# Down weight sums in whole rows of tiles behind two steps of each recurrent head, token sums in the gate's tile, operand parts in one tile

## The chip, the cores and the metric

The kernel runs on one core of a Trainium2 chip. The metric is the device time of one execution in microseconds, from three runs whose median is given. The core has TensorE (matrix products into PSUM), VectorE (DVE in the rows), ScalarE (ACT), GpSimd (POOL) and SyncE (SP), whose queue issues nearly all DMAs of this kernel. Each engine takes its instructions in the order in which the program holds them.

## The reference

One layer of a streaming encoder, for 1024 prompt tokens and 64 sample tokens, 1088 together, width 1024. The inputs are projected by `w_in`; eight recurrent heads (HGRN2) and eight differential-attention heads work on the projections; a gated mix, a norm, a convolutional feed-forward part and a second norm follow.

```python
hq, hf, hi, hog, dq, dk, dv, g_hg, g_da = _split_in(x @ w_in)
f = lb_hk + (1.0 - lb_hk) * jax.nn.sigmoid(hf)        # forget gate
s_new, o = _hgrn2(q, 1.0 - f, hi, log(f), hg_s0)      # S_t = diag(f_t) S_{t-1} + k_t v_t^T, o_t = S_t^T q_t
y_hg = _rms_norm(o, hg_norm_g) * jax.nn.sigmoid(hog)
y_da = _rms_norm(_diff_attend(dq, dk, dv, lam, mask), subln_g) * (1.0 - lam_init)
m = jax.nn.sigmoid(g_hg) * (y_hg @ w_br_hg) + jax.nn.sigmoid(g_da) * (y_da @ w_br_da)
h = _layer_norm(DEEPNORM_ALPHA * x + m @ w_out, ln1_g, ln1_b)
up = h @ w_up                                         # 1024 -> 2 x 2816
val, gate = jnp.split(conv_b + sum(conv_w[j] * buf[:, j:j + T] for j in range(3)), 2, axis=-1)
out = _layer_norm(DEEPNORM_ALPHA * h + (jax.nn.silu(gate) * val) @ w_down, ln2_g, ln2_b)
```

## The kernel before

Every float32 product is computed as three products of rounded parts: an operand is split into a high part (`ScalarE`, a cast) and a low part (`VectorE`, a subtraction), lines 85 and 86 for weights, and high x high, high x low and low x high are accumulated in PSUM (lines 181, 154 and 1225). A weight load `wraw` is 128x512 in one of three buffers.

The work runs in stages. First x is read and transposed (`load_x`). Then the eight recurrent heads run in a loop (`hgrn`): four projections each (L181), decay factors at four block levels (`lvl`), a base level, whose last VectorE step is L435 (Qp times q), the copies of the base products into `att` (L441), the state products U (L463), the states (L471), the outputs (L490, L493), a norm, and the output gate, whose last VectorE step is L508; the head's output is stored by L509. TensorE works on the next head's projections while a head's chain of VectorE, ScalarE and GpSimd steps runs.

The products `up` and `down` of the feed-forward part use a scheme with seven products of half-size blocks instead of eight. It needs sums and differences of weight blocks and of token blocks. For `down` the four weight combinations named 5, 7, 6 and 3 are made ahead, in `down_sums`, and kept in scratch memory in HBM (`s_w`). There are 22 blocks of 128x256: per block four loads into `ws` tiles (four buffers), four VectorE operations (L525, L527, L529, L532), four stores. After each of the first six heads up to four blocks are called; `tc.issue_after(last.ins)` ties their DMAs in SyncE's queue behind the head's store L509, since the context ties only the instructions on the engine of the instruction it is given. The fourth load of a block follows the block's third store in the program.

After the attention heads and the mix comes `ffn`. Feature tiles f = 0 and 1 are computed as plain products; the tiles from 2 on by `seven_products`, whose results go into a tile `u` (two buffers) through `put` (L166, L168). `conv` reads `u`, writes two `c` tiles (two buffers): `val` and `gate`. Its first lines call `edges`, in which GpSimd zeroes and fills the edge columns of `u` (L1075, L1077). Then the product of the two is stored in `s_act`, and token differences are made for `down`: for f below 11 one difference is written into the first half of `u` and stored in `s_t` (L1130, L1135).

`down` takes its operands through `parts`: a load from scratch memory into the low part's tile, a cast (L1180), a subtraction (L1181); high and low parts are two tags of 15 buffers each, allocated after the 16 result tiles `z`.

The order of instructions on each engine is not written by hand: a planner at build time runs the program on a modelled timeline, takes what is ready by its place in the program, and adds a wait wherever a tile or its memory is reused. `issue_after` adds an order without a wait. Pools that follow one another share memory; `reuse_waits="tile"` makes a new tile wait for those old tiles only whose addresses it takes.

Of the kernel before, what the change touches and what calls it, by code (L numbers as in the profile page):

```python
# [10 lines left out]
F32 = mybir.dt.float32  # L11
F32R = mybir.dt.float32r
I32 = mybir.dt.int32
AF = mybir.ActivationFunctionType
ALU = mybir.AluOpType
# [5 lines left out]
P = 128  # L21
# [5 lines left out]
H = 8  # L27
DFF = 2816
NF = DFF // P
# [16 lines left out]
HF, HT, HD = NF // 2, T // 2, D // 2  # L46
# [7 lines left out]
class K:  # L54
# [282 lines left out]
    def hgrn(self, h, mm, sc, xs, hp, w0=None):  # L337
        nc, a, o = self.nc, self.a, self.o
        w = a["w_in"][0]
        c = h * P  # L340
        V, S, G = nc.vector, nc.scalar, nc.gpsimd
# [92 lines left out]
        G.tensor_tensor(X, X, k, ALU.mult)  # L434
        V.tensor_tensor(Qp, Qp, q, ALU.mult)  # L435
        for g in range(2):
# [70 lines left out]
        V.scalar_tensor_tensor(oT, oT, self.hgg, sq, ALU.mult, ALU.mult)  # L507
        V.tensor_tensor(oT, oT, gt, ALU.mult)  # L508
        return nc.sync.dma_start(self.s_yh[c:c + P, :], oT)  # L509


    def down_sums(self, hp, blocks):
        nc, V = self.nc, self.nc.vector
        w = self.a["w_down"][0]
        CW = HD // 2
        for n in blocks:
            rows, cols = slice(n // 2 * P, n // 2 * P + P), slice(n % 2 * CW, n % 2 * CW + CW)

            def load(i, j):
                t = hp.tile([P, CW], F32, tag="ws", name=self.nm("ws"), bufs=4)  # L520
                r0, c0 = j * HF * P + n // 2 * P, i * HD + n % 2 * CW
                nc.sync.dma_start(t, w[r0:r0 + P, c0:c0 + CW])
                return t
            a21, a22, a11 = load(1, 0), load(1, 1), load(0, 0)
            V.tensor_tensor(a22, a21, a22, ALU.add)  # L525
            nc.sync.dma_start(self.s_w["5"][rows, cols], a22)
            V.tensor_tensor(a21, a11, a21, ALU.subtract)  # L527
            nc.sync.dma_start(self.s_w["7"][rows, cols], a21)
            V.tensor_tensor(a11, a22, a11, ALU.subtract)  # L529
            nc.sync.dma_start(self.s_w["6"][rows, cols], a11)  # L530
            a12 = load(0, 1)
            V.tensor_tensor(a12, a12, a11, ALU.subtract)  # L532
            nc.sync.dma_start(self.s_w["3"][rows, cols], a12)

# [301 lines left out]
    def run(self, stop=99):  # L836
# [3 lines left out]
        with top:  # L840
# [25 lines left out]
            if True:  # L866
                with ExitStack() as es:
# [20 lines left out]
                    for h in range(self.dbg.get("nh", H) if stop != 2 else 0):  # L888
                        last = self.hgrn(h, mm, sc, xs, hp, w0 if h == 0 else None)
                        if h < H - 1:  # L890
                            with tc.issue_after(last.ins):
                                self.down_sums(hp, range(4 * h, min(4 * h + 4, 2 * HF)))
            if stop < 2:
# [162 lines left out]
    def ffn(self):  # L1056
# [11 lines left out]
        def new_u(f):  # L1068
            u = up.tile([P, 2, W], F32, tag="u", name=self.nm("u"), bufs=2)
            return u  # L1070

        def edges(f, u):
            for i in range(2):
                j = f + i * NF
                G.memset(u[:, i, 0:2], 0.0)  # L1075
                for r in range(2):
                    G.tensor_copy(u[:, i, TP + 2 + r:TP + 3 + r],  # L1077
                                  par[:, self.o_st + r * 44 + j:self.o_st + r * 44 + j + 1])

        def put(u, c):  # L1080
# [18 lines left out]
        def weights(f):  # L1099
            return self.seven_weights(a["w_up"][0], f * P, (f + NF) * P)  # L1100

        def conv(f, u):
            c = []
            edges(f, u)
            for i in range(2):
# [22 lines left out]
            def less(dst, src):  # L1128
                for sl, vs in pieces:
                    V.tensor_tensor(dst[:, sl], val[:, vs], src[:, sl], ALU.subtract)  # L1130

            t2, t3 = (u[:, i, :HT] for i in range(2))
            if f < HF:
                less(t2, val)
                nc.sync.dma_start(self.s_t["5"][r], t2)  # L1135
                return
            nc.sync.dma_start(t2, self.s_t["5"][r])
# [39 lines left out]
        def parts(n, f, hi, lo):  # L1177
            raw = lo.bitcast(F32)
            nc.sync.dma_start(raw, operand(n, f))
            S.copy(hi, raw)  # L1180
            V.tensor_tensor(lo, raw, hi.bitcast(F32), ALU.subtract)  # L1181
            return hi, lo
        for f in range(2, NF):
            u, w = new_u(f), weights(f)
            self.seven_products([(w, self.xop[c], put(u, c)) for c in range(2)], up)
            conv(f, u)
            if f == NF - 2:
                for i, e in enumerate(early):
                    parts("1", i, *e)
# [76 lines left out]
        both = ((0, QW), (QW, QW))  # L1266

        z = {n: [ap.tile([P, HT], F32, name=f"z{n}{j}") for j in range(HJ)] for n in ("11", "22", "12", "21")}
        later = []
        for n in DOWN:  # L1270
            x = list(early) if n == "1" else []
            for f in range(len(x), HF):
                x.append(parts(n, f, *[ap.tile([P, HT], F32R, tag="o" + t, name=self.nm("o" + t), bufs=15)
                                       for t in "hl"]))
            if n == "4":
# [77 lines left out]
```

## Time and profile before

| | us |
|---|---|
| median of three runs (lowest to highest) | 2369.62 (2367.26 to 2377.26) |
| the profiled execution | 2376.17 |
| its span, first to last instruction | 2374.3 |
| TensorE busy in the span | 2310.8 |
| VectorE, ScalarE, GpSimd busy | 1578.8, 1061.2, 514.5 |
| mean granted clock of TensorE, as a share of full speed | 0.992 |

Times in rows are microseconds unless marked ns. A stretch row gives from:to, its length, the busy time and count of instructions of PE (matrix products), PEld (weight loads of TensorE), DVE, ACT and POOL, the granted TensorE clock as a share of 2.4 GHz, the busy share of the DMA engines and GB/s moved. A row of waits gives engine and line, what ended the wait, total, number of times, longest. A row by line gives the shape and count, then busy us and mean ns of one, then the engine's idle time just before, with what ended it. A row in order of time gives start, length, engine, line, what was written from what, and in brackets the idle time before it with its end. A row of DMAs gives the number, KB of each and median us from issue to landing. A busy TensorE is not TensorE at its peak, since ends of products are modelled; spans on GpSimd are rough.

### The profile page before, as it was taken

The page shows a single profiled execution, that of the slowest core. Times are in us where ns is not written, and L with a number is a line of the kernel's source. Part 1 is how long each engine was busy: PE and PEld are TensorE (multiplying, and loading weights), DVE is VectorE, ACT ScalarE, POOL GpSimd, SP SyncE. Part 2 cuts the span into 40 slices and gives each one's busy share as a digit, 9 for nine tenths or more (in the row PEclk, how much of TensorE's full clock was granted, in tenths as well). Part 3 has the DMA queues.
Part 4 walks back from the last instruction along what each step waited for, and adds up shares of the span by engine and source line. Part 5 has one row for each costly group of instructions (what it writes and reads, how often), then busy time and mean ns, then how long its engine had stood idle before and what let it go on. Part 6 is the DMA issues. An engine that isn't in the chain of part 4 may idle for free.

```text
span 2374.3 us, 42425 instructions
## 1 busy us (share of the span) xinstructions
PE 2310.8 (97%) x16270; PEld 2254.5 (95%) x16270; DVE 1578.8 (66%) x2788; ACT 1061.2 (45%) x1929; POOL 514.5 (22%) x576
## 2 busy tenths in 40 slices
PE   8999999999999999999999999999999999999998
PEld 8989998999999999999999899999999999999998
DVE  3675655776376655556556756568998888885667
ACT  3444443444344444344344744335644444454346
POOL 2222212222331211201201000012454444410001
PEclk9999999999999999999999999999999999999999
DMA  4132323321433323323323767444433345567665
GB/s 129 35 113 88 98 83 103 111 82 45 135 119 106 98 78 85 92 77 102 91 78 108 240 191 220 136 133 141 149 115 110 100 136 162 161 210 231 214 201 163
DMA packets 389234, 300.83 MB, mean 127 GB/s; under 512 B 23739, under 2 KB 358231, under 8 KB 389030
## 3 DMA queue, kind: packets, MB, share of 16 engines
q1 hardware_dynamic: 384294, 293.36, 40.7%
q10 hardware_dynamic: 4224, 4.46, 0.5%
q8 instruction: 128, 2.10, 0.4%
q0 software_dynamic: 512, 0.29, 0.1%
q14 instruction: 76, 0.62, 0.1%
HBM read 203.70 MB, written 81.75 MB: 120 GB/s over the span
## 4 chain that ended last, share of the span: by engine, by line
PE 80%; DVE 6%; DMA 5%; ACT 3%; issue 3%; POOL 1%; SPq 1%; DVEq 0%; POOLq 0%; ACTq 0%
PE mm L181 40%; PE mm L154 17%; PE mm L1225 10%; PE s L668 3%; PE av L709 2%; DMA ws<-w_down 2%; PE wt L703 1%; DMA s_w<-ws 1%; DMA gb<-s_g 1%; DVE wlo L86 1%; PE o L490 1%; DMA ydl<-s_yd 1%; PE nat L333 1%; PE o L493 1%; PE lv L407 1%
## 5 line engine op out<-in xcount | busy, mean ns | idle before, releaser
L181 PE MATMUL mm<-x,whi 128*128 128x362 f32 (+1 forms) x3456 | 878.2, 333 | 5.4 <-DMA wraw<-w_in 2.4
L181 PEld LDWEIGHTS mm<-x,whi 128*128 128x128 f32 x3456 | 614.3, 190 | 10.9 <-ACT x L311 4.8
L181 PE MATMUL mm<-x,wlo 128*128 128x362 f32 (+1 forms) x1728 | 573.1, 333 | 0.0
L86 DVE TENSOR_TENSOR wlo<-wraw,whi 128x512 fp32r<-128x512 f32 (+1 forms) x420 | 308.6, 740 | 194.5 <-ACT whi L85 190.7
L85 ACT CAST whi<-wraw 128x512 fp32r<-128x512 f32 (+1 forms) x420 | 254.7, 611 | 404.7 <-PE mm L181 197.3
L181 PEld LDWEIGHTS mm<-x,wlo 128*128 128x128 f32 x1728 | 328.0, 190 | 2.0 <-issue 1.0
L1225 PE MATMUL mm<-ol,whi 128*128 128x272 f32 (+2 forms) x608 | 174.6, 289 | 1.1 <-DVE ol L1181 1.1
L1225 PE MATMUL mm<-oh,wlo 128*128 128x272 f32 (+2 forms) x608 | 174.0, 288 | 0.0
L1225 PE MATMUL mm<-oh,whi 128*128 128x272 f32 (+2 forms) x608 | 172.8, 290 | 1.0 <-ACT oh L1180 1.0
L1225 PEld LDWEIGHTS mm<-ol,whi 128*128 128x128 f32 x608 | 114.3, 188 | 1.3 <-DVE ol L1181 1.3
L1225 PEld LDWEIGHTS mm<-oh,whi 128*128 128x128 f32 x608 | 113.3, 188 | 1.2 <-ACT oh L1180 1.2
L1225 PEld LDWEIGHTS mm<-oh,wlo 128*128 128x128 f32 x608 | 114.3, 188 | 0.0
L559 POOL TENSOR_TENSOR rs<-rs,mhalf 128x4 f32<-128x4 f32 (+1 forms) x24 | 22.5, 939 | 373.5 <-DVE rs L558 373.5
L595 POOL TENSOR_TENSOR KL<-kT,B 64x512 fp32r<-64x512 f32 x32 | 48.8, 1526 | 218.2 <-DVE B L594 193.5
L85 ACT CAST whi<-wsum 128x512 fp32r<-128x512 f32 x80 | 49.5, 620 | 95.6 <-PE mm L154 75.0
L668 PE MATMUL s<-B,A 128*128 128x512 f32 (+3 forms) x384 | 87.7, 354 | 3.4 <-ACT E L689 1.6
L168 DVE TENSOR_TENSOR u<-mm,p 128x272 f32<-128x272 f32 (+2 forms) x160 | 55.0, 367 | 45.3 <-PE mm L154 44.2
L387 POOL TENSOR_TENSOR P<-X,k 128x544 f32<-128x544 f32 (+1 forms) x32 | 56.0, 1754 | 129.8 <-ACT X L381 84.6
L704 ACT COPY wT<-wt 128x512 f32<-128x512 f32 (+1 forms) x96 | 46.3, 482 | 80.9 <-PE wt L703 80.3
L709 PE MATMUL av<-dvn,wT 128*128 128x128 f32 x576 | 80.0, 275 | 1.3 <-ACT wT L704 1.3
L1113 DVE SCALAR_TENSOR_TENSOR c<-u,par,c 128x1090 f32<-128x1090 f32 x44 | 79.3, 1802 | 0.7 <-ACT c L1110 0.4
L181 PE MATMUL mm<-ydh,whi 128*128 128x272 f32 x256 | 74.2, 291 | 3.7 <-ACT whi L85 3.7
(392 smaller groups left out, 5986.7 us busy)
## 6 DMA issues: line engine op xcount, KB each, us to landing
wraw<-w_in SPq DMA_DIRECT2D x144, 256.0 KB, 2.9
wraw<-w_up SPq DMA_DIRECT2D x124, 256.0 KB, 3.2
wraw<-w_br_hg SPq DMA_DIRECT2D x48, 256.0 KB, 3.7
ol<-s_t SPq DMA_DIRECT2D x44, 272.0 KB, 5.3
ws<-w_down SPq DMA_DIRECT2D x88, 128.0 KB, 2.9
s_w<-ws SPq DMA_DIRECT2D x88, 128.0 KB, 2.3
s_act<-c SPq DMA_DIRECT2D x22, 512.0 KB, 3.4
s_t<-u SPq DMA_DIRECT2D x33, 272.0 KB, 3.2
```

Source lines behind the costliest of these rows:

```text
L85: nc.scalar.copy(hi[:, :kn, :], raw[:, :kn, :])
L86: nc.vector.tensor_tensor(lo[:, :kn, :], raw[:, :kn, :], hi[:, :kn, :].bitcast(F32), ALU.subtract)
L154: nc.tensor.matmul(ps, l, r, start=(first and k == 0 and i == 0), stop=(k == 3 and i == 2), skip_group_check=not first)
L168: V.tensor_tensor(dst, ps[:, sl], d[other][:, sl], ALU.add)
L181: nc.tensor.matmul(ps[:, :cw], l, r[:, :cw], start=(k == 0 and i == 0), stop=(k == n - 1 and i == 2))
L387: G.tensor_tensor(pk, xv[:, :, :hb], blocks(k, B)[:, :, :hb], ALU.mult)
L595: G.tensor_tensor(kl[r], kT[r, sl], b[r, m, :].bitcast(F32), ALU.subtract)
L668: nc.tensor.matmul(dst[:, kc * 512:kc * 512 + kw], A[i // 2][:, p, m, qc], B[kc][:, m, :kw], start=(p == 0), stop=(p == 1))
L704: S.copy(wT[:, g * 4:g * 4 + nb, :], ps[:, :nb * P].rearrange("p (n e) -> p n e", e=P))
L709: self.last_av = nc.tensor.matmul(av[:, i % n4, :], wT[:, kb, :], vn[:, kb, :], start=(kb == 0), stop=(kb == i))
L1113: V.scalar_tensor_tensor(t[:, :W - 2], u[:, i, 1:W - 1], par[:, self.o_w1 + j:self.o_w1 + j + 1], t[:, :W - 2], ALU.mult, ALU.add)
L1225: nc.tensor.matmul(ps, l, r[:, c0:c0 + cw], start=(k == 0 and i == 0), stop=(k == HF - 1 and i == 2))
```

## The change

Three things are edited. `down_sums` works on a row of 128x512 tiles instead of 128x256 blocks, 11 rows; the four loads stand first, the four adds are made under `issue_after` of a VectorE step, and the four stores follow. `hgrn` returns two such steps, `mid` (the product L435) and `end` (the product L508); the first row of a head is tied behind `mid`, the second behind `end`. The DMAs are no longer tied. In `ffn` the edge columns of `u` are filled where the tile is made, which is now before the preceding convolution, and for f below 11 the token difference is written into the gate's `c` tile and not into `u`. In `down` the high and low parts of an operand share one tile of 15 buffers, and the result tiles `z` are allocated after the first operands.

```diff
--- before.py
+++ after.py
@@ -432,7 +432,7 @@
         S.activation(Qp, X, AF.Exp)
         S.activation(X, X, AF.Exp, scale=-1.0)
         G.tensor_tensor(X, X, k, ALU.mult)
-        V.tensor_tensor(Qp, Qp, q, ALU.mult)
+        mid = V.tensor_tensor(Qp, Qp, q, ALU.mult)
         for g in range(2):
             ps = sc.tile([P, 4, P], F32, tag="sc", name=self.nm("bs"))
             for i in range(4):
@@ -505,32 +505,29 @@
             S.activation(sq[:, c0:c0 + cw], ms[:, :cw], AF.Ln, bias=self.eps)
         S.activation(sq, sq, AF.Exp, scale=-0.5)
         V.scalar_tensor_tensor(oT, oT, self.hgg, sq, ALU.mult, ALU.mult)
-        V.tensor_tensor(oT, oT, gt, ALU.mult)
-        return nc.sync.dma_start(self.s_yh[c:c + P, :], oT)
-
-
-    def down_sums(self, hp, blocks):
+        end = V.tensor_tensor(oT, oT, gt, ALU.mult)
+        nc.sync.dma_start(self.s_yh[c:c + P, :], oT)
+        return mid, end
+
+
+    def down_sums(self, hp, n, behind):
+
         nc, V = self.nc, self.nc.vector
         w = self.a["w_down"][0]
-        CW = HD // 2
-        for n in blocks:
-            rows, cols = slice(n // 2 * P, n // 2 * P + P), slice(n % 2 * CW, n % 2 * CW + CW)
-
-            def load(i, j):
-                t = hp.tile([P, CW], F32, tag="ws", name=self.nm("ws"), bufs=4)
-                r0, c0 = j * HF * P + n // 2 * P, i * HD + n % 2 * CW
-                nc.sync.dma_start(t, w[r0:r0 + P, c0:c0 + CW])
-                return t
-            a21, a22, a11 = load(1, 0), load(1, 1), load(0, 0)
+        rows = slice(n * P, (n + 1) * P)
+        t = {}
+        for i, j in ((1, 0), (1, 1), (0, 0), (0, 1)):
+            t[i, j] = hp.tile([P, HD], F32, tag="ws", name=self.nm("ws"), bufs=4)
+            r0 = j * HF * P + n * P
+            nc.sync.dma_start(t[i, j], w[r0:r0 + P, i * HD:(i + 1) * HD])
+        a11, a21, a12, a22 = t[0, 0], t[1, 0], t[0, 1], t[1, 1]
+        with self.tc.issue_after(behind.ins):
             V.tensor_tensor(a22, a21, a22, ALU.add)
-            nc.sync.dma_start(self.s_w["5"][rows, cols], a22)
             V.tensor_tensor(a21, a11, a21, ALU.subtract)
-            nc.sync.dma_start(self.s_w["7"][rows, cols], a21)
             V.tensor_tensor(a11, a22, a11, ALU.subtract)
-            nc.sync.dma_start(self.s_w["6"][rows, cols], a11)
-            a12 = load(0, 1)
             V.tensor_tensor(a12, a12, a11, ALU.subtract)
-            nc.sync.dma_start(self.s_w["3"][rows, cols], a12)
+        for k, x in (("5", a22), ("7", a21), ("6", a11), ("3", a12)):
+            nc.sync.dma_start(self.s_w[k][rows], x)
 
 
     def gates(self, mm, gp, js):
@@ -886,10 +883,9 @@
                         G.memset(t, 0.0)
                         self.att.append(t)
                     for h in range(self.dbg.get("nh", H) if stop != 2 else 0):
-                        last = self.hgrn(h, mm, sc, xs, hp, w0 if h == 0 else None)
-                        if h < H - 1:
-                            with tc.issue_after(last.ins):
-                                self.down_sums(hp, range(4 * h, min(4 * h + 4, 2 * HF)))
+                        steps = self.hgrn(h, mm, sc, xs, hp, w0 if h == 0 else None)
+                        for n, behind in zip(range(2 * h, min(2 * h + 2, HF)), steps):
+                            self.down_sums(hp, n, behind)
             if stop < 2:
                 return
             mm = top.enter_context(tc.tile_pool(name="mm_d", bufs=2, space=PSUM, reuse_waits="tile"))
@@ -1067,15 +1063,13 @@
 
         def new_u(f):
             u = up.tile([P, 2, W], F32, tag="u", name=self.nm("u"), bufs=2)
-            return u
-
-        def edges(f, u):
             for i in range(2):
                 j = f + i * NF
                 G.memset(u[:, i, 0:2], 0.0)
                 for r in range(2):
                     G.tensor_copy(u[:, i, TP + 2 + r:TP + 3 + r],
                                   par[:, self.o_st + r * 44 + j:self.o_st + r * 44 + j + 1])
+            return u
 
         def put(u, c):
             def f(row, half):
@@ -1101,7 +1095,6 @@
 
         def conv(f, u):
             c = []
-            edges(f, u)
             for i in range(2):
                 j = f + i * NF
                 G.tensor_copy(cst[:, 0:2, j], u[:, i, TP:TP + 2])
@@ -1128,12 +1121,12 @@
             def less(dst, src):
                 for sl, vs in pieces:
                     V.tensor_tensor(dst[:, sl], val[:, vs], src[:, sl], ALU.subtract)
+            if f < HF:
+                less(gate, val)
+                nc.sync.dma_start(self.s_t["5"][r], gate[:, :HT])
+                return
 
             t2, t3 = (u[:, i, :HT] for i in range(2))
-            if f < HF:
-                less(t2, val)
-                nc.sync.dma_start(self.s_t["5"][r], t2)
-                return
             nc.sync.dma_start(t2, self.s_t["5"][r])
             nc.sync.dma_start(t3, self.s_act[r, HT:T])
             less(t2, t2)
@@ -1180,10 +1173,13 @@
             S.copy(hi, raw)
             V.tensor_tensor(lo, raw, hi.bitcast(F32), ALU.subtract)
             return hi, lo
+        u = new_u(2)
         for f in range(2, NF):
-            u, w = new_u(f), weights(f)
+            w = weights(f)
             self.seven_products([(w, self.xop[c], put(u, c)) for c in range(2)], up)
-            conv(f, u)
+
+            u, done = new_u(f + 1) if f < NF - 1 else None, u
+            conv(f, done)
             if f == NF - 2:
                 for i, e in enumerate(early):
                     parts("1", i, *e)
@@ -1264,14 +1260,15 @@
         def tiles(c0, cw):
             return [(r, min(P, c0 + cw - r)) for r in range(c0, c0 + cw, P)]
         both = ((0, QW), (QW, QW))
-
-        z = {n: [ap.tile([P, HT], F32, name=f"z{n}{j}") for j in range(HJ)] for n in ("11", "22", "12", "21")}
         later = []
         for n in DOWN:
             x = list(early) if n == "1" else []
             for f in range(len(x), HF):
-                x.append(parts(n, f, *[ap.tile([P, HT], F32R, tag="o" + t, name=self.nm("o" + t), bufs=15)
-                                       for t in "hl"]))
+                t = ap.tile([P, 2, HT], F32R, tag="o", name=self.nm("o"), bufs=15)
+                x.append(parts(n, f, t[:, 0], t[:, 1]))
+            if n == "1":
+
+                z = {n: [ap.tile([P, HT], F32, name=f"z{n}{j}") for j in range(HJ)] for n in ("11", "22", "12", "21")}
             if n == "4":
                 break
             for j in range(HJ):
```

## Rows read from the trace of the kernel before

**Rows 1.** The page, busy time of each engine over the whole span.

```profile
PE 2310.8 (97%) x16270; PEld 2254.5 (95%) x16270; DVE 1578.8 (66%) x2788; ACT 1061.2 (45%) x1929; POOL 514.5 (22%) x576
```

**Rows 2.** Busy time by stretch: recurrent heads, the products of up, those of down.

```profile
126.00:478.00 352.00, 333.56 (x2203) 320.16 (x2202) 230.21 (x361) 147.81 (x202) 78.46 (x39) 0.98 0.33 100
40.00:126.00 86.00, 85.54 (x566) 83.58 (x565) 44.93 (x64) 37.71 (x49) 19.69 (x9) 1.00 0.14 40
478.00:640.00 162.00, 160.14 (x1053) 155.69 (x1052) 90.74 (x133) 71.17 (x100) 40.29 (x23) 0.99 0.25 76
1735.00:2120.00 385.00, 385.00 (x3064) 385.00 (x3063) 328.82 (x509) 169.43 (x256) 159.92 (x253) 1.00 0.42 133
2130.00:2350.00 220.00, 220.00 (x1759) 219.77 (x1758) 145.89 (x261) 105.70 (x206) 4.99 (x10) 1.00 0.70 220
```

**Rows 3.** Who waited for whom, TensorE, 125 to 530 us.

```profile
PE U L463 <- DVE att L441: 9.8, 3, 5.0
PE nat L333 <- DVE vT L348: 7.9, 10, 2.0
```

**Rows 4.** Groups by line, VectorE, 125 to 530 us.

```profile
L525 DVE TENSOR_TENSOR ws<-ws,ws 128x256 f32<-128x256 f32 x22 | 13.7, 623 | 26.8 <-DMA ws<-w_down 20.1 <-issue 6.7
L527 DVE TENSOR_TENSOR ws<-ws,ws 128x256 f32<-128x256 f32 x22 | 9.1, 416 | 3.6 <-DMA ws<-w_down 2.7 <-DVE att L420 0.7 <-DVE ws L525 0.2
L379 DVE TENSOR_TENSOR X<-b 128x512 f32<-128x512 f32 x6 | 4.1, 690 | 0.1
```

**Rows 5.** Instructions in order of time, VectorE and TensorE, around 170 us.

```profile
169.67 0.43 DVE L525 TENSOR_TENSOR ws<-ws,ws 128x256 f32<-128x256 f32 x1 [4.75 <-DMA ws<-w_down]
172.00 2.07 PE L463 MATMUL U<-vn,kn 128*128 128x128 f32 x8 [4.99 <-DVE att L441]
```

**Rows 6.** Busy time by stretch, right after four gaps of TensorE.

```profile
172.00:178.00 6.00, 6.00 (x23) 5.37 (x24) 4.72 (x14) 0.00 (x0) 0.00 (x0) 0.51 0.41 125
317.80:321.20 3.40, 3.40 (x14) 3.40 (x15) 3.29 (x10) 0.00 (x0) 0.00 (x0) 0.51 0.39 131
366.00:369.20 3.20, 3.20 (x15) 3.02 (x14) 1.96 (x6) 0.00 (x0) 1.34 (x1) 0.53 0.83 227
577.00:580.40 3.40, 3.40 (x16) 3.40 (x16) 3.40 (x5) 0.00 (x0) 0.00 (x0) 0.54 0.00 0
```

**Rows 7.** Busy time by stretch: from one end step to the last state step.

```profile
126.00:177.00 51.00, 45.19 (x298) 42.64 (x297) 42.10 (x66) 19.27 (x29) 10.40 (x5) 0.94 0.40 122
```

**Rows 8.** DMA issues on the page, KB each, median us to landing.

```profile
wraw<-w_in SPq DMA_DIRECT2D x144, 256.0 KB, 2.9
ws<-w_down SPq DMA_DIRECT2D x88, 128.0 KB, 2.9
s_w<-ws SPq DMA_DIRECT2D x88, 128.0 KB, 2.3
```

**Rows 9.** Who waited for whom, ScalarE, 125 to 530 us.

```profile
ACT whi L85 <- PE mm L181: 39.0, 24, 5.5
```

**Rows 10.** Instructions in order of time, SyncE's queue and TensorE, at the start.

```profile
11.64 1.88 SPq L71 DMA_DIRECT2D wraw<-w_in  x2
24.09 0.53 PE L181 MATMUL mm<-x,whi 128*128 128x362 f32 x1 [2.38 <-DMA wraw<-w_in]
```

**Rows 11.** Instructions in order of time, three engines, 1706 to 1714 us.

```profile
1706.33 0.39 PE L154 MATMUL mm<-t3h,whi 128*128 128x272 f32 x1 [1.36 <-DVE p L161]
1711.75 1.30 ACT L1110 ACTIVATE c<-u,par 128x1090 f32<-128x1090 f32 x1 [1.48 <-DMA s_act<-c]
1712.43 0.10 POOL L1075 MEMSET u<- 128x2 f32 x1 [1.55 <-DMA s_t<-u]
1713.37 0.39 PE L154 MATMUL mm<-b11h,whi 128*128 128x272 f32 x1 [2.25 <-ACT u L166]
```

**Rows 12.** Busy time by stretch: after that gap, and where down begins.

```profile
1713.40:1717.40 4.00, 4.00 (x20) 4.00 (x21) 4.00 (x11) 1.35 (x3) 4.00 (x8) 0.57 0.14 44
2120.00:2130.00 10.00, 7.93 (x61) 7.49 (x61) 10.00 (x14) 8.22 (x13) 0.00 (x0) 1.00 1.00 349
```

## The prediction

> **What bounds the kernel now.** Read the page's busy times first: TensorE is busy for 2310.8 us of the 2374.3 us span [rows 1], so all that a reordering can win is some 63 us of TensorE's idle time, plus whatever it loses at its lower clock level. The second view is the table by stretch, to see where that idle time lies. In the stretch from 126 to 478 us, five heads, TensorE is busy for 333.56 of 352 us, 18.44 idle; in the recurrent work before and after it (40 to 126, 478 to 640 us), where few or no Down sums run, it idles 0.46 + 1.86 = 2.32 us in 248. In the long runs of the up and the down products (385 and 220 us) it idles nothing at all [rows 2]. So nothing done inside those two runs can help, and what can help sits in the recurrent heads and at the two seams.
>
> Third, the waits. In the heads TensorE waits 9.8 us for VectorE's copy into att and 7.9 us for its vT copies [rows 3]. Fourth, the groups by line say what VectorE was doing: the first of the four Down sums, L525, has 26.8 us of VectorE's idle time in front of it, 20.1 of it for its loads from w_down [rows 4]. VectorE takes its instructions in the order in which they stand, so a sum whose rows have not landed holds up the recurrence behind it. Fifth, the order in time shows one such case whole: L525 sat for 4.75 us on a load at 169.67, and TensorE's U product then started after a gap of 4.99 us [rows 5]. After the larger gaps the granted clock falls: 0.51, 0.51 and 0.53 after three gaps in this stretch (mostly the 1.2 GHz level instead of 2.4), and 0.54 after one in a head without sums [rows 6].
>
> **The change part by part.**
>
> *Down sums.* The loads lose their place behind the head's last store. Only the four adds are now tied, and only in VectorE's queue: one set behind L435, one behind L508. A set's loads may go out as soon as the four ws tiles are free, that is when the set before it has been stored. Half a head, some 30 to 40 us, lies between two sets; a store lands in 2.3 us and a load in 2.9 [rows 8], so I expect no add to wait for a load. What that wins: the 18.44 us idle less what the clean heads would have in as long a stretch, 352 x 2.32/248 = 3.3, is 15.1 us. The clock: (1-0.51) x 6.0 + 0.49 x 3.4 + 0.47 x 3.2 = 6.1 us lost after gaps here, less the clean share 0.46 x 3.4 x 352/248 = 2.2 [rows 6], is 3.9 us.
>
> What it adds: 44 adds of 128x512 at 0.69 us (L379 has that shape) replace 88 of 128x256 at 0.42 to 0.62 [rows 4], so VectorE's work falls from about 42 to 30 us. But four adds in a row behind L508 hold the next head's first differences for 4 x 0.69 = 2.8 us, in five heads. At worst all of it reaches TensorE, 14 us; at best none. In the stretch of one head VectorE is busy 42.1 of 51 us and TensorE 45.2 [rows 7]; taking out sixteen sums of 0.42 us and putting back 2.8 leaves VectorE 38.2, so 7 us of product work still covers it. I take 0.4 us a head, 2 us. The set behind L435 falls where VectorE waits for TensorE anyway; if that cover is gone, it delays the att copy by up to 2.8 us in each of six heads, 17 us, and I take nothing, as the adds stand later in the program than the head's own steps and fill gaps. Together -15.1 - 3.9 + 2 = -17 us. Bounds: -19 with no burst cost, -4 when most of the two burst costs come through.
>
> The DMAs count too: 44 loads and 44 stores of 256 KB replace 88 and 88 of 128 KB, same bytes; a 256 KB load lands in the same 2.9 us as a 128 KB one [rows 8], so SyncE's queue has half as many issues. Weight loads of the heads stand in that queue behind stores that wait for adds. ScalarE's weight split waits for TensorE (39.0 us, 24 times) and not for a load in these heads [rows 9], so weights lie ready and I cost it at nothing; without that cover it is the slower rival below.
>
> The first set has nothing before it, so its four loads (1.05 MB) may go out while the inputs are still arriving. There a weight load issued at 11.64 us was used at 24.09, TensorE having waited 2.38 us for it [rows 10], 12 us instead of 2.9. This load's tile is free from the start and stands earlier in the program, so the new loads go behind it: 0 us; if ahead, 1.05 MB at the 133 GB/s of the up stretch [rows 2] is 7.9 us. The Trainium skill (DMA: Bandwidth & Descriptors, Queues, rings and completion order) says that each DMA engine consumes its descriptors in ring order; that 12 us landing agrees, and by this rule four loads put ahead cost the weight load their whole transfer, -13.6 instead of -21.5 in the sum below.
>
> *First token sums in the gate's tile, edges one step earlier.* At the seam into the paired products TensorE stands 1.36 us and 2.25 us; the second time it waits for a copy into u, while POOL waits for the store s_t from u, and ScalarE for a c tile [rows 11]. The next 4 us run at 0.57, 1.7 us lost [rows 12]. With the sum in the gate's tile, u is free once the convolution has read it, before that store. But the gate's c tile is now held for two subtractions and a store (2.3 to 2.9 us, rows 8), and the second convolution's ScalarE step waits for a c tile already. Gain at most 1.36 + 2.25 + 1.7 = 5.3 us; loss, if the held tile is what ScalarE stands at ahead of the copy, up to 4 us (store and subtractions). I take 2.25 + 1.7 less 1 for the held tile: -3. After that TensorE has no gap to win, and POOL, 160 of 385 us busy there [rows 2], has room for the earlier edges: 0.
>
> *Operand parts in one tile, z afterwards.* In 2120 to 2130 us TensorE is busy 7.93 us, VectorE 10.00 [rows 12]. The operand tiles move to the lowest addresses, over operands of the last up product that are read first, so their loads can start before that product ends. Gain at most 2.07 us, loss as much if an early load holds the queue. I take -1.5.
>
> **Sum.** -17 - 3 - 1.5 = -21.5 us on the profiled execution, 2376.2 to 2354.7; that execution lies 6.6 us above the median of the runs, so 2348 us. Its own range: -29 (all three gains whole, clean heads without clock dips) to -13, 2341 to 2357.
>
> **Rivals.**
>
> *The waits stay, in part.* A clean head still shows a gap followed by 0.54 [rows 6], and the bursts cost. If half the gain in the heads comes (-8.5) and the seams give 1.5, the time is 2376.2 - 10 - 6.6 = 2360 us. For: VectorE is the busiest engine behind TensorE there. Against: 26.8 us of its standing still goes [rows 4].
>
> *The change doesn't separate loads from adds.* If the adds of one set run just ahead of the next gate, store and load (2.3 + 2.9 = 5.2 us) lie between them and VectorE stands as before, eleven times. Then only the seams gain: 2365 to 2370 us. Against: half a head between the gates.
>
> *The first loads go ahead of the weights at the start.* It decides in which order SyncE's queue takes them: if the four loads stand before the one issued at 11.64 us, TensorE's wait of 2.38 us [rows 10] grows by the 7.9 us worked out above, and the time is 2348 + 8 = 2356 us. For: they wait for nothing. Against: they stand late in the program.
>
> *Slower: SyncE's queue.* Each set's stores wait in SyncE's queue for adds behind a late VectorE step, with the heads' weight loads behind them. It decides once the queue stands longer than the weights are ahead. Then every set costs a landing of 2.9 us [rows 8] and the two passes of the split, as long as a 128x512 add of 0.69 us [rows 4], 4.3 x 11 = 47 us, less 21.5: +25, 2395 us. Against: the split never waited for a load [rows 9], though stores waited for sums in that queue then too.
>
> **How the numbers follow.** Forecast 0.50, waits stay 0.20, first loads ahead 0.08, no separation 0.12, slower 0.10. A change under 0.5% (12 us) can hardly be told from none in this kernel, whose three runs lie 10 us apart. 2357.8 us is the border for faster: the forecast's case, two thirds of the first loads' and a little of the waits' make 0.57; slower is the last case less the part that stays under 2381.5 us, 0.09; the rest 0.34. The range 2338 to 2368 holds the forecast, the waits' and the first loads' cases and half of no separation.
>
> **What would show it.** Right: VectorE's idle time ahead of the first sum under 3 us instead of 26.8; TensorE's wait for att under 3 instead of 9.8; those five heads with less than 6 us idle; the gap of 2.25 at the up seam gone; 2120 to 2130 full. Wrong: sums that still wait for loads; splits that wait for wraw; a longer wait for the third weight tile at the start; a new gap at the second convolution's first step; the copies of vT late behind four adds in a row.

## The result, and the profile after

The changed kernel takes 2356.71 us (median of 5 runs, 2352.85 to 2360.26), the kernel before 2371.3 us (median of 5, 2367.26 to 2377.26): ratio 0.9936, 95% interval 0.9915 to 0.9956. It is faster, by 14.6 us. Forecast was 2348 us, with a range of 2338 to 2368. The profiled executions, 2376.2 us before and 2356.7 after, lie 19.5 us apart: that of before is 5 us above its kernel's median, that of after is on it. The page's first row, after, answers to [rows 1]:

```profile
PE 2303.1 (98%) x16270; PEld 2247.3 (95%) x16270; DVE 1579.6 (67%) x2744; ACT 1056.8 (45%) x1925; POOL 507.9 (22%) x576
```

The same 16270 matmuls take 7.7 us less, at a higher clock; the other 11.7 of the 19.4 us by which the span is shorter were idle time.

The heads first. Busy time by stretch, after (stretch, its length, then busy time and instructions of TensorE, its weight loads, VectorE, ScalarE, GpSimd, then TensorE's clock, DMA share, GB/s):

```profile
126.00:478.00 352.00, 345.29 (x2324) 334.54 (x2323) 244.71 (x335) 157.19 (x214) 80.52 (x41) 1.00 0.32 100
478.00:640.00 162.00, 158.42 (x1031) 153.15 (x1030) 83.72 (x119) 62.00 (x94) 50.34 (x33) 0.98 0.26 80
2101.00:2111.00 10.00, 7.92 (x61) 7.49 (x60) 9.71 (x13) 8.03 (x12) 0.00 (x0) 1.00 0.99 344
```

The 18.44 us idle of [rows 2] are 6.71, and the clock there is 1.00 instead of 0.98. The end of the last recurrent head, told by the first kT transposition behind it, comes at 624.01 us instead of 641.66: 17.65 us of the 19.5. Who waited, TensorE, and the sums by line, VectorE, both 125 to 530 us:

```profile
PE nat L333 <- DVE vT L348: 7.4, 11, 0.8
```

```profile
L528 DVE TENSOR_TENSOR ws<-ws,ws 128x512 f32<-128x512 f32 x10 | 10.5, 1050 | 0.2
L525 DVE TENSOR_TENSOR ws<-ws,ws 128x512 f32<-128x512 f32 x10 | 6.8, 682 | 0.0
```

The wait for att of [rows 3] is gone, and so are the 26.8 us ahead of the first sum [rows 4]. What stays is the wait for vT, in small pieces. The order in time around one head's end shows why; VectorE, then TensorE:

```profile
202.27 0.68 DVE L525 TENSOR_TENSOR ws<-ws,ws 128x512 f32<-128x512 f32 x1
...
205.35 0.68 DVE L526 TENSOR_TENSOR ws<-ws,ws 128x512 f32<-128x512 f32 x1
...
209.02 0.52 DVE L348 COPY vT<-mm 128x364 f32<-128x364 f32 x1
209.47 0.68 DVE L527 TENSOR_TENSOR ws<-ws,ws 128x512 f32<-128x512 f32 x1
...
211.34 0.52 DVE L348 COPY vT<-mm 128x362 f32<-128x362 f32 x1
211.78 1.40 DVE L528 TENSOR_TENSOR ws<-ws,ws 128x512 f32<-128x512 f32 x1
...
213.71 0.52 DVE L348 COPY vT<-mm 128x362 f32<-128x362 f32 x1
```

```profile
211.91 0.55 PE L333 MATMUL nat<-ident,vT 128*128 128x128 f32 x3 [0.77 <-DVE vT L348]
214.28 0.66 PE L333 MATMUL nat<-ident,vT 128*128 128x128 f32 x4 [0.57 <-DVE vT L348]
```

All four adds of the second set stand ahead of the last copy of vT, and each transposition waits for its copy.

The seams, where one stage meets the next, gave nothing. At the up seam (TensorE; ScalarE; SyncE's queue), the answer to [rows 11]; L1103 is the first step of the convolution, L1110 before, and L1115 the store of s_act:

```profile
1687.01 0.40 PE L154 MATMUL mm<-t3h,whi 128*128 128x272 f32 x1 [1.37 <-DVE p L161]
...
1714.47 0.36 PE L154 MATMUL mm<-t4h,whi 128*128 128x272 f32 x1 [1.54 <-DVE u L168]
...
1753.81 0.39 PE L154 MATMUL mm<-t3h,whi 128*128 128x272 f32 x1 [1.30 <-DVE p L161]
```

```profile
1711.29 1.30 ACT L1103 ACTIVATE c<-u,par 128x1090 f32<-128x1090 f32 x1 [5.43 <-DMA s_act<-c]
...
1714.70 1.30 ACT L1103 ACTIVATE c<-u,par 128x1090 f32<-128x1090 f32 x1 [1.32 <-DMA s_t<-c]
```

```profile
1693.59 13.42 SPq L97 DMA_DIRECT2D wraw<-w_up  x3
1707.10 0.46 SPq L1115 DMA_DIRECT2D s_act<-c  x1
```

The gap of 2.25 us is gone, with the low clock behind it (1.00 from 1680 to 1760 us, 0.98 before); gaps of 1.54 and 1.30 us (and one of 0.21) have come. Together the gaps are 4.4 us, 3.6 before. ScalarE now stands 5.43 us for a store that left SyncE's queue at 1707.10, behind three weight loads that waited for their tiles. At the down seam (TensorE) nothing has moved: 2.07 us idle in 10 before [rows 12], 2.08 after, in the same two gaps. TensorE before, then after:

```profile
2122.33 0.77 PE L1225 MATMUL mm<-oh,whi 128*128 128x272 f32 x4 [0.99 <-ACT oh L1180]
2124.18 0.39 PE L1225 MATMUL mm<-ol,whi 128*128 128x272 f32 x1 [1.08 <-DVE ol L1181]
```

```profile
2103.41 0.77 PE L1221 MATMUL mm<-o,whi 128*128 128x272 f32 x4 [0.99 <-ACT o L1173]
2105.26 0.40 PE L1221 MATMUL mm<-o,whi 128*128 128x272 f32 x1 [1.09 <-DVE o L1174]
```

### The profile page after: what moved, and what is told of

The parts are those of the page before. It is cut to its first block, busy times and chain, and to the rows that moved or that the text cites. A ratio compares the mean times of both kernels' runs of the same rounds, so it can differ in the third digit from the quotient of the medians.

```text
span 2354.9 us, 42194 instructions
## 1 busy us (share of the span) xinstructions
PE 2303.1 (98%) x16270; PEld 2247.3 (95%) x16270; DVE 1579.6 (67%) x2744; ACT 1056.8 (45%) x1925; POOL 507.9 (22%) x576
## 4 chain that ended last, share of the span: by engine, by line
PE 82%; DVE 6%; DMA 3%; issue 2%; ACT 2%; POOL 2%; SPq 0%; POOLq 0%; DVEq 0%; ACTq 0%
PE mm L181 43%; PE mm L154 15%; PE mm L1221 10%; PE s L665 3%; PE av L706 3%; PE lv L407 1%; PE wt L700 1%; DVE wlo L86 1%; PE nat L333 1%; DMA gb<-s_g 1%; PE o L490 1%; DMA ydl<-s_yd 1%; PE o L493 1%; PE avd L751 1%; POOL sg L363 1%
## 5 line engine op out<-in xcount | busy, mean ns | idle before, releaser
L1221 PE MATMUL mm<-o,whi 128*128 128x272 f32 (+2 forms) x1216 | 231.2, 289 | 2.1 <-DVE o L1174 1.1
L1221 PEld LDWEIGHTS mm<-o,whi 128*128 128x128 f32 x1216 | 191.0, 188 | 2.6 <-DVE o L1174 1.3
L1221 PE MATMUL mm<-o,wlo 128*128 128x272 f32 (+2 forms) x608 | 174.6, 288 | 0.0
L1221 PEld LDWEIGHTS mm<-o,wlo 128*128 128x128 f32 x608 | 114.2, 188 | 0.0
L665 PEld LDWEIGHTS s<-B,A 128*128 128x128 f32 x384 | 65.9, 190 | 12.1 <-DVE wlo L86 2.1
L102 POOL TENSOR_TENSOR wsum<-wraw,wraw 128x512 f32<-128x512 f32 x40 | 69.1, 1727 | 36.2 <-DVE wlo L86 35.2
```

Source lines behind the costliest of these rows:

```text
L102: G.tensor_tensor(t, x, y, op)
L665: nc.tensor.matmul(dst[:, kc * 512:kc * 512 + kw], A[i // 2][:, p, m, qc], B[kc][:, m, :kw], start=(p == 0), stop=(p == 1))
L1221: nc.tensor.matmul(ps, l, r[:, c0:c0 + cw], start=(k == 0 and i == 0), stop=(k == HF - 1 and i == 2))
```

## The experiments

Each was timed in turns with the kernel before on the same chip; a ratio is to that kernel, with its 95% interval. "Heads" is TensorE's busy time in the 352 us from 126 to 478 (333.56 before, 345.29 changed). A product at the lower clock is busy for longer, so where the clock of that stretch differs it is given too. The planner orders all steps anew for each kernel; no run holds the rest of its order fixed.

**One part at a time.** The Down sums alone (their two functions and the call, as in the diff):

> The kernel before with the Down sums of the change alone; the convolution and the operand tiles as before. Theory: nearly the whole gain of the change is made in the recurrent heads, 17 to 18 us by the end of head 7 as in the profile of the changed kernel, so about 2354 to 2357 us against 2371, and the changed kernel's other two parts are worth 0. Rival: the other two parts gave some of it (3 + 1.5 us, as forecast), or took some back; then this kernel is 3 us or more away from the changed one's 2356.7, above or below.

Measured: 2355.05 us, 0.9918 (0.9906 to 0.9930), heads 345.33. The whole gain: no less than the whole change's.

The convolution's edits alone (`less(gate, val)` and `new_u` a step earlier):

> The kernel before with the first token sums in the gate's tile and the earlier edges alone. Theory: 0, 2371 plus or minus 2 us: the gap of 2.25 us behind the copy into u goes, but two others of 1.3 to 1.5 us come, because ScalarE's first convolution step waits for the store s_act, which stands in SyncE's queue behind a third weight load, and VectorE's work piles up behind it. Rival, as forecast: the held tile costs 1 us only, 3 us are won, 2368.

Measured: 2375.38 us, 1.0008 (0.9997 to 1.0019). TensorE's waits, 1660 to 1775 us, of this kernel:

```profile
PE mm L154 <- DVE u L168: 3.3, 2, 3.1
PE mm L154 <- DVE p L161: 2.7, 2, 1.4
```

Before, it waited there 2.3 us for u and 1.4 for p. The waits have changed their lines and grown by 2.3 us, and the clock falls behind the longest of them, 3.15 us up to 1726.57:

```profile
1726.00:1730.00 4.00, 3.43 (x17) 3.46 (x18) 4.00 (x7) 1.70 (x3) 2.85 (x2) 0.58 0.00 0
```

No gain, as the theory said, but the new gap is longer than the 1.3 to 1.5 us that it named: ScalarE stood 7.03 us for the store of s_act here.

The operand tiles alone (`t[:, 0], t[:, 1]`, z behind them):

> The kernel before with the operand parts in one tile and z allocated afterwards alone. Theory: 0, the seam into the Down products keeps its two gaps (0.99 and 1.09 us in the changed kernel), since the operand loads leave SyncE's queue right behind three weight loads in either kernel. Rival, as forecast: earlier loads close both gaps, 1.5 to 2 us.

Measured: 2371.27 us, 0.9988 (0.9979 to 0.9997). TensorE is busy for 37.93 of the 40 us from 2100, 37.94 before: the seam is the same. The interval ends just under 1, but nothing in the trace answers to it; I count the part as 0.

**Where the second set stands.**

```
-        return mid, end
+        return mid, states          # states = the add into st[:, 9], the last state step
```

> The changed kernel with the second set of sums of each head tied behind the last state step instead of behind the head's last product with the gate. Theory: the adds no longer stand between the copies of vT; the pairs of gaps of 0.77 and 0.57 us there (five heads) fall to the 0.5 to 0.7 us of the heads without sums, so 3 to 5 us less than the changed kernel, about 2352 to 2354. Rival 1: the gaps only move, the four adds now delay the copies into sg of the next head: no difference. Rival 2: later landing of the stores keeps weights back in SyncE's queue: slower by some us, with splits that wait for wraw.

Measured: 2351.98 us, 0.9910 (0.9896 to 0.9923). The stretch and TensorE's wait in 125 to 530:

```profile
126.00:478.00 352.00, 348.57 (x2339) 338.13 (x2338) 241.82 (x333) 159.35 (x215) 88.05 (x43) 1.00 0.30 95
```

```profile
PE nat L333 <- DVE vT L348: 4.1, 6, 0.7
```

The theory's mechanism holds in the trace: 3.3 us less idle, the wait for vT 4.1 instead of 7.4, and no wait of TensorE that takes its place. The second gap in each head was the price of the place. The times agree (2352.0 against 2356.7), though the two intervals overlap.

**No tie at all.** `with self.tc.issue_after(behind.ins)` taken from the adds:

> The changed kernel with the adds tied to nothing: whole rows, loads and adds as early as the order allows, which puts all eleven sets from the first transposes to about head 2. Theory: the tie is what keeps a set's adds half a head away from its loads; without it each set follows the one before with a store (2.1 us) and a load (4.0 us) between, so VectorE stands 3 to 6 us before most first sums again and TensorE's waits come back in heads 0 to 2: slower than the changed kernel by 10 to 30 us, 2367 to 2385. Rival: only the loads' freedom counts, not where the adds stand: within 3 us of 2356.7.

Measured: 2367.11 us, 0.9983 (0.9973 to 0.9992): 10 us slower than the change. The sums now fall into the start and the first heads; VectorE, 0 to 640 us:

```profile
DVE ws L525 <- DMA ws<-w_down: 21.9, 8, 5.9
```

The adds follow their loads at once, and VectorE stands for them again. TensorE loses time where the sums now crowd: it is busy for 81.12 of the 86 us from 40 to 126 (85.54 in the changed kernel) and for 69.02 of the 74 us behind them (72.66). The tie is worth about 10 us.

**Loads and adds together, whole rows.** As before the change, the transfers are tied behind the head's last store, and the adds follow by their data alone:

```
-  for n, behind in zip(range(2 * h, min(2 * h + 2, HF)), steps):
-      self.down_sums(hp, n, behind)
+  with tc.issue_after(steps):          # steps = the head's store to s_yh
+      for n in range(2 * h, min(2 * h + 2, HF)):
+          self.down_sums(hp, n)        # adds inside not tied further
```

> The changed kernel with whole rows, but loads and adds both tied behind the head's last store, as in the kernel before. Theory: the separation of loads from adds made the gain, not the size of the tiles: VectorE's idle time ahead of the first sum (26.8 us before) comes back for eleven sets instead of 22, some 10 to 20 us of it, and TensorE's wait for att too; 2362 to 2370. Rival: whole rows alone (half as many transfers and adds) made the gain: within 3 us of 2356.7.

Measured: 2354.94 us, 0.9933 (0.9921 to 0.9945), heads 345.72. My theory falls: without any separation the gain is all there, and VectorE's idle time ahead of the sums is 0.0 to 0.2 us. Its adds, one head:

```profile
201.83 2.31 SPq L521 DMA_DIRECT2D ws<-w_down  x4
```

```profile
208.37 0.68 DVE L524 TENSOR_TENSOR ws<-ws,ws 128x512 f32<-128x512 f32 x1
```

Four loads leave at once, and the first add stands 6.5 us behind the first, without a wait.

**Half rows, loads free.** The change's ties, tiles of 128x256:

```
+  t[i, j] = hp.tile([P, CW], F32, tag="ws", ..., bufs=8)   # CW = HD // 2; two sets of four, eight adds behind the same step
```

> The changed kernel with its ties and free loads, but tiles of 128x256 again, in eight buffers: 88 adds and 88 loads and stores instead of 44. Theory: with loads apart from adds, size matters little: eight adds of 0.42 us instead of four of 0.69 are 0.6 us more of VectorE a set, at most 7 us in all and mostly hidden; 2356 to 2360. Rival: whole rows made the gain, by fewer transfers in SyncE's queue: 2365 or more.

Measured: 2374.02 us, 1.0006 (0.9996 to 1.0016): nothing gained, heads 338.04. That looked like the rival, but not by transfers: no sum waits for a load here either. TensorE's wait, 125 to 530 us:

```profile
PE nat L333 <- DVE vT L348: 15.8, 12, 1.9
```

Eight adds of 0.41 to 0.65 us stand where four of 0.68 to 1.05 stood, and what they delay is vT. The longer waits, up to 1.9 us, have the low clock behind them (0.50 from 216.2 to 220 us, after two of them), so that the stretch runs at 0.97 instead of 1.00:

```profile
126.00:478.00 352.00, 338.04 (x2224) 325.90 (x2224) 221.72 (x363) 157.74 (x209) 97.63 (x39) 0.97 0.32 98
```

TensorE gets 100 products fewer done in it than in the changed kernel: 7 us are lost to waits, and by estimate some 10 (0.03 of 352 us) by the clock. So the next kernel has half rows and the second set at the state steps (both edits above):

> Tiles of 128x256 in eight buffers, loads free, as in half_rows_separate (2374.0), but each head's second set, now eight adds, tied behind the last state step. Theory: what half rows lost was not the size of the transfers but eight adds standing ahead of the copies of vT (17.0 us of TensorE's waits for them, 8.6 with four); with the set at the state steps that wait falls to about 5 us and the time to 2354 to 2360. Rival: the size itself costs (twice as many transfers and adds): 2366 or more, with the waits elsewhere.

Measured: 2352.4 us, 0.9917 (0.9904 to 0.9931; one of five executions, at 6846 us, is left out), heads 348.58. Wait for vT:

```profile
PE nat L333 <- DVE vT L348: 4.1, 6, 0.7
```

The same as whole rows in that place. The size of the tiles and the number of transfers are worth nothing that shows; where the adds stand is worth 21.6 us between these two kernels, waits and clock together.

**Four tiles or eight.** Then what held the kernel before? In one of its heads VectorE takes the four first sums so:

```profile
140.16 0.41 DVE L525 TENSOR_TENSOR ws<-ws,ws 128x256 f32<-128x256 f32 x1
...
148.65 0.43 DVE L525 TENSOR_TENSOR ws<-ws,ws 128x256 f32<-128x256 f32 x1 [1.40 <-DMA ws<-w_down]
...
157.93 0.43 DVE L525 TENSOR_TENSOR ws<-ws,ws 128x256 f32<-128x256 f32 x1 [1.21 <-DMA ws<-w_down]
```

and the fourth at 169.67 [rows 5]. Each block waits for the one before it to leave the four tiles, some 10 us a link. In three of the six heads the last link falls on the att copies: these are the three waits of [rows 3]. The kernel before with one number changed:

```
-  t = hp.tile([P, CW], F32, tag="ws", name=self.nm("ws"), bufs=4)
+  t = hp.tile([P, CW], F32, tag="ws", name=self.nm("ws"), bufs=8)
```

> The kernel before with eight tiles of 128x256 for the Down sums instead of four, nothing else: loads and adds tied together behind the head's last store as before. Theory: what the kernel before lost was the chain of each head's four blocks through four tiles (load, sum, store, load), not the tie and not the size; with eight tiles two blocks load at once, so VectorE's idle time ahead of the first sum falls from 26.8 us to under 5, as with whole rows tied the same way, and the time to 2353 to 2360. Rival: half rows tied so cost as before, 2368 to 2373, and whole rows are needed.

Measured: 2357.4 us, 0.9928 (0.9914 to 0.9942), heads 342.98. First sums and the att copy of the same head:

```profile
140.39 0.41 DVE L525 TENSOR_TENSOR ws<-ws,ws 128x256 f32<-128x256 f32 x1
141.99 0.41 DVE L525 TENSOR_TENSOR ws<-ws,ws 128x256 f32<-128x256 f32 x1
...
152.33 0.41 DVE L525 TENSOR_TENSOR ws<-ws,ws 128x256 f32<-128x256 f32 x1
153.94 0.41 DVE L525 TENSOR_TENSOR ws<-ws,ws 128x256 f32<-128x256 f32 x1
...
158.49 0.40 DVE L532 TENSOR_TENSOR ws<-ws,ws 128x256 f32<-128x256 f32 x1
...
165.01 1.64 DVE L441 COPY_PREDICATED att<-bm,bs 128x512 f32<-128x512 int32 x2 [0.70 <-PE bs L440]
```

Two links instead of four, the last add (L532) done 6 us ahead of att, and no sum waits for a load (26.8 us of idle time ahead of the first sums before, 0.0 here). This one number gives what the change gives: its whole rows in four tiles hold the bytes of eight half rows.

**The seams.**

```
+  q = S if f < 2 else nc.sync                      # stores of s_act
+  (G if n == "1" and f >= EARLY else nc.sync)      # queue of the operand loads of the first Down product
```

> The changed kernel with two kinds of transfers taken out of SyncE's queue: the first two stores of s_act go out from ScalarE's queue, and the operand loads of the first Down product from GpSimd's. Theory: at both seams SyncE's order held the forecast's gain back, a store behind three weight loads at the up seam, operand loads behind three weight loads at the down seam; then ScalarE's wait of 5.4 us for s_act falls to about 3 and TensorE's gap of 1.5 us behind it goes, and the two gaps of 0.99 and 1.09 us in front of the Down products go: 3 us less than the changed kernel at most, seen in the trace, at the edge of what the times show. Rival: the tiles come free that late, or VectorE is full there: the gaps stay. Second rival: loads by GpSimd's queue land later than SyncE's, and the gaps at the down seam grow.

Measured: 2362.6 us, 0.9955 (0.9941 to 0.9968), some 5 us slower than the change, with intervals that just overlap. At the up seam the store is early, ScalarE's wait for it 1.02 us instead of 5.43, and the gap at 1714.47 is gone; gaps of 1.37, 0.79 and 1.61 us are left, 3.8 together instead of 4.4. ScalarE now stands 2.01 us for the gate's tile and its store, where it stood 1.32. SyncE's order was one cause there, and 0.6 us of gaps its price here. At the down seam GpSimd's queue issued the first nine loads at 2097.09, where SyncE's queue issued the first at 2099.52 in the changed kernel, so their tiles were free 2.4 us earlier; but they land later, and TensorE's gaps there are 2.89, 0.86 and 2.69 us. The issues, this kernel (KB each, median us to landing):

```profile
o<-s_act SPq DMA_DIRECT2D x22, 272.0 KB, 5.1
o<-s_act POOLq DMA_DIRECT2D x10, 272.0 KB, 6.8
```

**What helped, together.** Two kernels. Without the convolution's edits, the second set at the state steps:

> The kernel before with the Down sums of the change, the second set tied behind the last state step, and the operand parts in one tile; the convolution as before. Theory: the gains add, as the places do not touch: second set 4.7 us under the changed kernel (2352.0 measured), and the convolution's part left out saves 1 to 2 us more: 2349 to 2352. Rival: the seam's two gaps and its lower clock come back and cost 2 us: 2354.

Measured: 2351.55 us, 0.9912 (0.9898 to 0.9926), heads 348.58. And the changed kernel with the second set at the state steps, the stores of s_act from ScalarE's queue, and other transfers moved out of the operand loads' way:

```
+  (q or nc.sync).dma_start(raw[:, :kn, :], ...)    # q = G for product "1", j > 1: weights, not operands
```

> The changed kernel with three edits: the second set of sums behind the last state step, the first two stores of s_act from ScalarE's queue, and the weight loads of the first Down product's third and fourth output tiles from GpSimd's queue, so that the operand loads in SyncE's queue stand behind nothing that waits. Theory: operand loads leave 2 us earlier, as from GpSimd's queue before, but land as fast as SyncE's do (5.1 us), so the two gaps of 0.99 and 1.09 us ahead of the Down products shrink to under 1 us together, and the up seam keeps the 0.7 us won; with the 4.7 us of the second set the time is 2349 to 2351. Rival: VectorE's split behind the last convolution is late as well and the gaps stay; 2351 to 2352.

Measured: 2350.39 us, 0.9902 (0.9889 to 0.9915), the lowest median, but not apart from the others with the second set at the state steps (2351.55 to 2352.4). Up seam: gaps of 1.37 and 0.87 us, 2.2 together, and no low clock behind them (1.00 from 1680 to 1760 us). Down seam (SyncE's queue; ScalarE; TensorE):

```profile
2084.05 5.13 SPq L1173 DMA_DIRECT2D o<-s_act  x6
```

```profile
2093.35 1.30 ACT L1103 ACTIVATE c<-u,par 128x1090 f32<-128x1090 f32 x1 [0.29 <-DVE u L168]
2094.55 3.37 ACT L1174 CAST o<-o 128x544 fp32r<-128x544 f32 x6
```

```profile
2095.23 0.78 PE L1222 MATMUL mm<-o,whi 128*128 128x272 f32 x4 [0.99 <-ACT o L1174]
2097.08 0.39 PE L1222 MATMUL mm<-o,whi 128*128 128x272 f32 x1 [1.07 <-DVE o L1175]
```

The operands leave 11 us ahead of the first product on them instead of 4, and both gaps are what they were. The rival holds: the first operand's split stands on ScalarE and VectorE behind the last convolution, which waits for the last copy into u. No run put the split ahead of that step, so whether the gaps would then close is not shown.

## Why the prediction was right, and where it was not

**Heads.** The size holds: -17 forecast, -17.65 by the end of the heads in the profiles, and the sums alone give the whole gain. By terms: idle without the burst, 18.44 - 3.43 (the 352 us with the second set at the states) = -15.0, against -15.1; burst 348.57 - 345.29 = +3.3, against +2; the rest, -5.9, is the clock and what lies outside that stretch, against -3.9 for the clock. The last two miss by 1.3 and 2.0 us in opposite directions, so the closeness of the sum is in part luck. The first set's place behind L435 costs nothing, as taken.

**The reason given for it** was wrong in part. I said that the gain comes from loads that no longer stand with their adds. Whole rows with their loads tied as before gain as much, half rows kept apart gain nothing where they stand, and eight tiles in the kernel before gain it all. Two things count: how many links the chain load, sum, store, load has in a head (four tiles made four links), and what the adds stand ahead of on VectorE. The rival "no separation", 2365 to 2370, went wrong by the same step: loads and adds together do not cost a store and a load each time.

**The signs named ahead.** VectorE's idle time ahead of the first sum is 0.0 us and TensorE's wait for att is gone, as named; the heads are 6.71 us idle where under 6 was named; the gap of 2.25 us is gone, but the place has new ones; 2101 to 2111, once 2120 to 2130, is not full. Of the signs of being wrong two came: vT late behind the four adds, +3.3 us where +2 was taken, and a wait at the second convolution's first step. No sum and no weight split of the heads waits for its load.

**Up seam.** The term -3 measured 0: the Down sums alone end where the whole change does, the convolution's edits alone at 1.0008. The copy into u is free as forecast. The step that failed is the sum "2.25 + 1.7 less 1 for the held tile", which leaves nothing else to wait for. The held gate's tile costs ScalarE 1.32 us, about the 1 taken; what had no term is the other c tile, val's. Its store to s_act leaves at 1707.10, 2.6 us behind its data and three weight loads, where before it left with its data, and ScalarE's wait for it became 5.43 us, 1.02 with the store in another queue. That alone does not bring the gain: with the early store the gaps are still 3.8 us, 3.6 before. What the rest of the seam's gaps come from, with VectorE busy for 72 of 80 us there, was only argued.

**Down seam.** The term -1.5 measured 0. The step that failed is "so their loads can start before that product ends": they leave 3.9 us ahead of the first product on them in both kernels, and where they leave 11 us ahead, the gaps stay. What is left as the bound is the order of ScalarE's and VectorE's work, which I had not looked at.

**Start.** Costed at 0, and 0: the event at 24.09 [rows 10] comes at 24.05, and for the reason given. SyncE's queue after, then ScalarE's split of the third weight tile, after and before:

```profile
11.74 0.38 SPq L71 DMA_DIRECT2D wraw<-w_in  x1
13.27 2.05 SPq L522 DMA_DIRECT2D ws<-w_down  x2
```

```profile
22.75 0.62 ACT L85 CAST whi<-wraw 128x512 fp32r<-128x512 f32 x1 [2.82 <-DMA wraw<-w_in]
```

```profile
22.79 0.62 ACT L85 CAST whi<-wraw 128x512 fp32r<-128x512 f32 x1 [0.98 <-DMA wraw<-w_in]
```

The load that is awaited is the first of the two of [rows 10]. It leaves ahead of the new loads and lands after 11.0 us, 11.1 before. Right behind its split ScalarE casts the part of x that TensorE goes on with; the profile now names that cast for TensorE's wait, which is 4.30 us long because the work ahead of it ended earlier. Only the second weight load, which now leaves at 17.51, has two of the new loads ahead of it, and its split does not wait for it: so the rival "first loads ahead" took place for a load that nobody awaited. The Trainium skill (DMA: Bandwidth & Descriptors, Queues, rings and completion order) says that each DMA engine consumes descriptors in ring order. From it came -13.6 for new loads ahead of the awaited one; that order did not come about, and no run here tests the rule.

**From the profile to the runs.** 2348 against 2356.7 is 8.7 us. Two come from the terms (-19.5 instead of -21.5). The other 6.6 are the step "that execution lies 6.6 us above the median": I carried this distance over to the changed kernel, whose profiled execution lies on its median. It may be that part of what made that execution slow, gaps and the clock behind them, is what the change removes, so that the distance could not stay; no run shows this apart.

## What to carry to other kernels

Where an engine stands for loads in the middle of other work, count first how many times a ring of tiles turns in that stretch: doubling the tiles here gave what a rewrite of loads, ties and sizes gave. Filler work in an engine's queue costs by what stands right behind it: moved from ahead of awaited copies to a place where TensorE does not wait for what stands behind them, the same adds gave 3.3 us of idle time back (5 us by the medians), and as eight halves 22, waits and clock together. Before a seam's gap is put down to transfers, read what the two engines that prepare the first operand are doing; an earlier load did not help a split that stands behind another step.

## What the runs showed of the hardware

The executions of one program differ, and TensorE's clock with them: of 23 runs of the kernel before, the three fastest (2367.1 to 2368.6 us) had a mean granted clock of 0.994, and the two with the lowest clock, 0.989 and 0.990, took 2377.6 and 2376.5. Of 2370 us, 0.005 is 12 us, about the distance between them. What a gap costs beyond its length differs from place to place: the clock was 0.57 behind the 2.25 us at the up seam before [rows 12], 0.58 behind 3.15 us with the convolution's edits alone, and 1.00 behind 1.54 us in the changed kernel (1714.4 to 1718.4 us).

The ten operand loads of 272 KB that GpSimd's queue issued landed in 6.8 us (median), as shown with that experiment; the same ten took 5.2 from SyncE's queue in the changed kernel. The other transfers around them were not the same, so this is not the queue's price alone. The whole rows of w_down, in the changed kernel:

```profile
ws<-w_down SPq DMA_DIRECT2D x44, 256.0 KB, 4.0
```

The half rows took 2.9 [rows 8], and I had expected 2.9 for both; it costs nothing here, as no add waits.
